# All of the short convolution in the paired products of a hybrid mixer block, six z tiles in its old place, time-step products among the first pairs

## The chip, the core and the metric

The kernel runs on one core of one Trainium2 chip. The metric is the device time of one launch in microseconds (us). TensorE (PE in the profile) does the matrix products, its weight loads are listed apart as PEld; VectorE (DVE), ScalarE (ACT) and GpSimd (POOL) do elementwise work; SyncE (SP) only issues DMA transfers. ACT and POOL can issue transfers as well. Each engine runs its own list of instructions in order, and waits on semaphores for the others.

## The reference

One layer over 1024 rows of 1024 channels, in float32: a mixer with two branches, then a feed-forward part (hidden size 2816), with normalisations. The mixer, cut to what matters:

```python
u = rmsnorm(x) @ w_in          # 1024 x 10272
z, xbc, dt_raw, s_b, s_c, s_x, g_a, g_b = split(u)   # 2048, 3072, 32, then 1024 each
xbc = silu(causal_conv4(xbc) + bias)            # x, B, C of the scan
dt  = softplus(dt_raw + dt_bias)                # "time steps", 32 heads
y   = ssd_scan(x, dt, a, B, C) + d_skip * x     # 32 heads in 4 groups
y   = group_rmsnorm(y * silu(z)) * ssd_norm_w
v   = causal_conv3(s_c * s_x)                   # the short convolution
merged = sigmoid(g_a) * (y @ w_ssd_proj) + sigmoid(g_b) * ((s_b * v) @ w_sconv_proj)
h = h + merged @ w_o
```

## The kernel before

**Products.** Every float32 operand is split into a high part (written by ACT) and a low part (the difference, written by DVE), and a product is three matmuls: high by high, high by low, low by high (`mm3`, `mmc`, lines 81 to 83 and 663 to 665). A weight slab of 128 columns is a page of 128 x 8 x 128; all large tiles are pages out of one pool of 47, and all product sums lie in eight banks of PSUM.

**First stage, pairs.** 29 pairs of 128-column tiles of `w_in` are computed by a scheme with seven products in place of eight (`Pair`, `ORDER`; its sums of operands are T1 to T4 on the activation side, S1 to S4 on the weight side). One product of one pair is a slot: twelve matmuls. The first three pairs (six z tiles) go product by product through 21 slots, while `second_half()` still makes the second half of the normalised rows and T1, T2, T3, B22 and T4 out of it; the table `turns` says behind which slot it takes a step. The other 26 pairs follow one after the other, a pair with a convolution of the scan's inputs and one of the list `free_p` by turns. Before, `free_p` holds nine pairs of the short convolution (channels 0 to 767 of s_c, s_x, s_b) and then five pairs of z. What follows a pair (silu, convolution, store to DRAM) is a generator in the list `side`, and `pump()` takes one step of one generator per slot. Copies between DRAM buffers for later stages (`v_sums`, and in the next stage `y_sums`, which also works on DVE) are generators in `aux`, taken by `pump_aux()`, here at every seventh slot.

**Time steps.** `steps_pe()` at slot 25 splits a small slab of 32 columns, makes the d_skip columns, and issues 60 matmuls into two banks; `time_steps` works on from there.

**Second stage, direct tiles and scan.** 22 tiles of 128 columns are computed plainly in `direct_tile`: two halves of 24 matmuls. Before, the first six are the last 256 channels of s_c, s_x and s_b, with their short convolution made on DVE and ACT out of PSUM; sixteen gate tiles follow, which ACT copies out of PSUM and stores by its own DMA queue. Between these matmuls the scan runs: 32 items (4 groups by 8 chunks of 128 rows), each with `part1` (transposes, decay matrix) and `part2` (products with the state), one step about every fifth group of matmuls. ACT makes the decay with Exp in `prep2` (line 390 on). The x rows of a half group are loaded by `want(.., 2)` (line 363) in `part1` of the last chunk before they are used. The slab of tile i + 2 is loaded at step (1, 0) of tile i; its high part is made at (0, 1) and its low part at (0, 7) of tile i + 1.

**Third stage on.** `Stream` runs the merge products in chunks: `ahead(loads, splits)` says how many chunks have been loaded and split. Then come the output product and the feed-forward part; the change leaves them alone.

Of the kernel before, what the change touches and what calls it, by code (L numbers as in the profile page):

```python
# [13 lines left out]
P = 128  # L14
# [25 lines left out]
def hybrid_block(ctx: ExitStack, tc: tile.TileContext, x, nmw, w_in, cw, cb, dtb, alog, dsk, snw,  # L40
# [186 lines left out]
    wdt_s = wslab(w_in, DT0, H)  # L227
# [396 lines left out]
    def conv_sb(j):  # L624
        def f(u):
            v = held.pop(j)
            V.tensor_mul(v, u, v)
# [290 lines left out]
    z_pairs = [Pair(i * P, (silu_z(i), silu_z(i + 1))) for i in range(0, 16, 2)]  # L918
# [3 lines left out]
    sc_pairs = [Pair(c0 + j * P, (f(j), f(j + 1))) for j in (0, 2, 4)  # L922
# [46 lines left out]
    direct = []  # L969
    for j in (6, 7):  # L970
        hold = {}

        def d_sc(ps, hf, hold=hold):
            if hf == 0:
                hold[0] = page("sc")
            nc.scalar.activation(hold[0][:, hf * 512:hf * 512 + 512], ps, AF.Copy)

        def d_sx(ps, hf, hold=hold, j=j):
            sc, o = hold[0], slice(hf * 512, hf * 512 + 512)
            V.tensor_mul(sc[:, o], ps, sc[:, o])  # L980
            if hf:
                v = hold[0] = page("v")
                nc.scalar.activation(v, sc, AF.Copy, scale=scc(2, j))
# [4 lines left out]
        def d_sb(ps, hf, hold=hold, j=j):  # L988
            v, o = hold[0], slice(hf * 512, hf * 512 + 512)
            V.tensor_mul(v[:, o], ps, v[:, o])  # L990
            if hf:
# [22 lines left out]
    def direct_tile(i):  # L1014
# [3 lines left out]
        for hf in range(2):  # L1018
            ps = bank("pr")
            for k in range(KT):  # L1020
# [15 lines left out]
                if i + 2 < len(direct) and (hf, k) == (1, 0):  # L1036
# [489 lines left out]
    for p in first[1:]:  # L1526
        p.y.load()
    for p in first:
        p.x.load()
    loaded[0] = NF  # L1530
    wdt_s.load()
# [36 lines left out]
    def second_half():  # L1568
# [19 lines left out]
        yield  # L1588
        for k in range(2):
# [3 lines left out]
        yield  # L1593
        every(put("B22", raw1[1]))
# [7 lines left out]

    gen = second_half()
# [104 lines left out]
```

## Time and profile before

| | |
|---|---|
| time of three runs | 1981.1, 1982.43 (median), 1985.02 us |
| profiled execution | 1979.01 us, span 1977.2 us |
| mean granted clock of TensorE | 0.984 |
| busy: PE, DVE, ACT, POOL | 1908.5, 1299.5, 960.8, 177.1 us |
| first pairs | about 20 to 110 us of the span |
| other pairs | about 110 to 617 us |
| direct tiles and scan | about 617 to 1006 us |

The page splits the span in 40 slices and gives the busy share of each engine in tenths, and the clock that TensorE was granted. Views of the trace give the same for any window, the waits of one engine by what ended them, the instructions in order of time, and the DMA issues. A wait row reads: engine, tile and line that waited, what it waited for, total us, number, longest. A group row reads: line, engine, operation, tiles and shapes, count, busy us, mean ns of one, and the idle time before.

### The profile page before, as it was taken

What the parts mean: (1) busy time and instruction counts of PE and PEld (TensorE: products, weight loads), DVE (VectorE), ACT (ScalarE), POOL (GpSimd) and SP (SyncE); (2) the same over time, 40 slices, a digit from 0 to 9 for tenths busy, and PEclk for the clock granted to TensorE, in tenths of its full rate; (3) what the DMA queues carried; (4) which work ended last, traced back from release to release, by engine and by line L of the source; (5) the groups of instructions that cost most, each with busy time, mean ns of one, the idle gap of its engine ahead of it and who ended that gap; (6) DMA issues with size and microseconds to landing.
All of it is one profiled execution on the core that took longest, in us unless ns stands there. A gap on an engine that the chain in (4) does not pass through costs nothing.

```text
span 1977.2 us, 24421 instructions
## 1 busy us (share of the span) xinstructions
PE 1908.5 (97%) x8917; PEld 1563.3 (79%) x8917; DVE 1299.5 (66%) x1678; ACT 960.8 (49%) x1526; POOL 177.1 (9%) x156
## 2 busy tenths in 40 slices
PE   6899999999999998999999999989999999999998
PEld 4678888888887876887878888878888888878886
DVE  6747878778765886887958557867444444455465
ACT  5534444444457766776546544355333333335433
POOL 0000101010100111111200000101121112100000
PEclk8899999999999998998999999999999999999999
DMA  5176989799975649687789866843989788868553
GB/s 175 35 202 156 234 228 238 206 245 249 257 214 181 187 151 276 229 255 234 249 312 406 289 213 207 219 139 80 237 190 207 209 195 194 211 236 306 199 183 116
DMA packets 350833, 422.49 MB, mean 214 GB/s; under 512 B 19752, under 2 KB 226424, under 8 KB 350712
## 3 DMA queue, kind: packets, MB, share of 16 engines
q1 hardware_dynamic: 305112, 356.95, 54.9%
q0 software_dynamic: 43296, 55.58, 17.6%
q10 hardware_dynamic: 2304, 8.39, 1.1%
q8 instruction: 70, 1.15, 0.2%
q14 instruction: 51, 0.42, 0.1%
HBM read 328.95 MB, written 145.24 MB: 240 GB/s over the span
## 4 chain that ended last, share of the span: by engine, by line
PE 58%; DVE 3%; DMA 1%; ACT 1%; issue 0%; SPq 0%; DVEq 0%; ACTq 0%
PE gb L664 5%; PE gb L665 5%; PE gb L663 5%; PE fb L665 4%; PE fb L664 4%; PE fb L663 4%; PE gd L665 4%; PE gd L664 4%; PE gd L663 4%; PE fd L665 3%; PE fd L663 3%; PE fd L664 3%; PE pr L81 3%; PE pr L83 3%; PE pr L82 3%; PE pdg L483 1%
## 5 line engine op out<-in xcount | busy, mean ns | idle before, releaser
L77 DVE TENSOR_TENSOR wl<-ws,wh 128x1024 fp32r<-128x1024 f32 (+1 forms) x78 | 94.4, 1211 | 123.2 <-ACT wh L76 123.2
L664 PE MATMUL gb<-ql,gh 128*128 128x512 f32 x432 | 169.6, 393 | 4.1 <-DVE ql L77 4.1
L663 PE MATMUL gb<-qh,gh 128*128 128x512 f32 x432 | 169.6, 393 | 3.2 <-ACT qh L76 3.2
L665 PE MATMUL gb<-qh,gl 128*128 128x512 f32 x432 | 169.0, 391 | 0.0
L83 PE MATMUL pr<-th,wl 128*128 128x512 f32 x352 | 139.9, 397 | 6.9 <-DVE wl L1011 6.9
L81 PE MATMUL pr<-th,wh 128*128 128x512 f32 x352 | 146.3, 416 | 0.0
L663 PE MATMUL fb<-th,wh 128*128 128x512 f32 x352 | 138.5, 393 | 2.6 <-ACT th L76 2.0
L82 PE MATMUL pr<-tl,wh 128*128 128x512 f32 x352 | 139.9, 397 | 0.0
L665 PE MATMUL fb<-th,wl 128*128 128x512 f32 x352 | 138.0, 392 | 0.8 <-DVE wl L77 0.8
L664 PE MATMUL fb<-tl,wh 128*128 128x512 f32 x352 | 138.2, 393 | 0.5 <-DVE tl L77 0.5
L663 PE MATMUL gd<-qh,gh 128*128 128x512 f32 x324 | 126.0, 389 | 0.0
L664 PE MATMUL gd<-ql,gh 128*128 128x512 f32 x324 | 126.0, 389 | 0.0
L665 PE MATMUL gd<-qh,gl 128*128 128x512 f32 x324 | 126.0, 389 | 0.0
L76 ACT ACTIVATE qh<-cb 128x1024 fp32r<-128x1024 f32 x98 | 100.0, 1020 | 39.2 <-PE gb L664 17.2
L77 DVE TENSOR_TENSOR ql<-cb,qh 128x1024 fp32r<-128x1024 f32 x98 | 115.6, 1180 | 2.4 <-ACT qh L76 2.1
L665 PE MATMUL fd<-th,wl 128*128 128x512 f32 x264 | 102.7, 389 | 0.0
L663 PE MATMUL fd<-th,wh 128*128 128x512 f32 x264 | 102.7, 389 | 0.0
L664 PE MATMUL fd<-tl,wh 128*128 128x512 f32 x264 | 102.7, 389 | 0.0
L74 DVE SCALAR_TENSOR_TENSOR gl<-ca,gh 128x1024 fp32r<-128x1024 f32 (+1 forms) x60 | 70.5, 1174 | 45.0 <-ACT gh L73 45.0
L664 PEld LDWEIGHTS gb<-ql,gh 128*128 128x128 f32 x432 | 81.8, 189 | 21.6 <-DVE ql L77 4.7
L663 PEld LDWEIGHTS gb<-qh,gh 128*128 128x128 f32 x432 | 81.9, 190 | 20.9 <-ACT qh L76 3.9
L665 PEld LDWEIGHTS gb<-qh,gl 128*128 128x128 f32 x432 | 81.8, 189 | 17.1
(310 smaller groups left out, 4711.3 us busy)
## 6 DMA issues: line engine op xcount, KB each, us to landing
ws<-in_w_in_dram SPq DMA_DIRECT2D x80, 512.0 KB, 7.8
ws<-in_w_gate_dram SPq DMA_DIRECT2D x77, 256.0 KB, 3.7
ws<-in_w_up_dram SPq DMA_DIRECT2D x77, 256.0 KB, 4.2
ca<-u_d SPq DMA_DIRECT2D x35, 512.0 KB
ab<-ac_d SPq DMA_DIRECT2D x32, 512.0 KB, 5.6
xbc_d<-cv SPq DMA_DIRECT2D x24, 512.0 KB, 3.4
ws<-ws POOLq DMA_DIRECT2D x22, 512.0 KB, 6.5
wd_d<-in_w_down_dram SPq DMA_DIRECT2D x20, 512.0 KB, 8.7
```

The lines of the kernel that those rows point to most:

```text
L74: nc.vector.scalar_tensor_tensor(lo, src, -1.0, hi.bitcast(F32), op0=ALU.mult, op1=ALU.subtract)
L76: nc.scalar.activation(hi, src, AF.Copy)
L77: nc.vector.tensor_sub(lo, src, hi.bitcast(F32))
L81: nc.tensor.matmul(o, lh, rh, start=first, stop=False)
L82: nc.tensor.matmul(o, lh, rl, start=False, stop=False)
L83: nc.tensor.matmul(o, ll, rh, start=False, stop=last)
L483: nc.tensor.matmul(pdg[64 * i:64 * i + 64, r * P:(r + 1) * P], xx[:, 0, 2 * r + i, :], ab[:, 2 * r + i, :], start=True, stop=True)
L663: nc.tensor.matmul(o, lh, rh, start=first, stop=False, skip_group_check=True)
L664: nc.tensor.matmul(o, lh, rl, start=False, stop=False, skip_group_check=True)
L665: nc.tensor.matmul(o, ll, rh, start=False, stop=last, skip_group_check=True)
```

## The change

- The list `free_p` now begins with all twelve pairs of the short convolution; the z pairs beyond the first three are cut from five to two. The copies `v_sums` are started from the pairs for both halves, and `pump_aux()` comes at every third slot instead of every seventh.
- The first six direct tiles are now z tiles 10 to 15 (`z_raw`): ACT applies Silu to each half straight out of PSUM and stores the tile by its own DMA queue.
- The slab of the time steps is loaded ahead of the first x slabs and split before slot 0; its 24 and 36 matmuls stand behind slots 5 and 11. `second_half()` makes B22 before T3. The d_skip columns move to slot 35.
- The slab of direct tile i + 2 is loaded at step (0, 2) instead of (1, 0), and the merge chunks are loaded and split one chunk sooner.

TensorE, first pairs. `pd_` tiles are sums of pairs, `ts_` is the sum of the time steps; `th`, `tl` are the parts of the activations. Before, behind slot 5:

```order
L663 MATMUL pd_541<-th_370,wh_378 128x512
L664 MATMUL pd_541<-tl_371,wh_378 128x512
L665 MATMUL pd_541<-th_370,wl_379 128x512
L663 MATMUL pd_559<-th_533,wk_495 128x512
L664 MATMUL pd_559<-tl_534,wk_495 128x512
L665 MATMUL pd_559<-th_533,wk_495 128x512
```

Now, at the same place:

```order
L663 MATMUL pd_545<-th_370,wh_378 128x512
L664 MATMUL pd_545<-tl_371,wh_378 128x512
L665 MATMUL pd_545<-th_370,wl_379 128x512
L663 MATMUL ts_563<-th_316,wdt_384 32x512
L664 MATMUL ts_563<-tl_317,wdt_384 32x512
L665 MATMUL ts_563<-th_316,wdt_385 32x512
```

24 rows of `ts` now stand ahead of the first row that reads T1 (`th_533` before), and 36 more ahead of slot 12.

ScalarE, first direct tile: `cd`, `ab` are the decay of the scan (Exp), `pr` is the sum of a direct tile, `st` the state of the scan. Before:

```order
L390 ACTIVATE cd_4634<-ab_4535 128x8
L392 ACTIVATE ab_4535<-ab_4535,pac 128x128 x8
L394 ACTIVATE ab_4535<-ab_4535 128x1024
L976 ACTIVATE sc_4655<-pr_4588 128x512
L476 ACTIVATE st_4666<-pst_4667 128x512
L430 ACTIVATE bh_4717<-pcb_4713 128x128
L434 ACTIVATE xw_4720<-xx_4716 128x512
L448 ACTIVATE y_4528<-bc_4530,cols 128x128 x2
L448 ACTIVATE y_4529<-x_561_4451,cols 128x128 x2
L390 ACTIVATE cd_4733<-ab_4607 128x8
```

Now:

```order
L390 ACTIVATE cd_4646<-ab_4544 128x8
L392 ACTIVATE ab_4544<-ab_4544,pac 128x128 x8
L394 ACTIVATE ab_4544<-ab_4544 128x1024
L975 ACT_TABLE_LOAD
L975 ACTIVATE gt_4667<-pr_4598 128x512
L476 ACTIVATE st_4676<-pst_4677 128x512
L430 ACTIVATE bh_4727<-pcb_4723 128x128
L434 ACTIVATE xw_4730<-xx_4726 128x512
L448 ACTIVATE y_4537<-bc_4539,cols 128x128 x2
L448 ACTIVATE y_4538<-x_562_4459,cols 128x128 x2
L390 ACT_TABLE_LOAD
L390 ACTIVATE cd_4743<-ab_4619 128x8
```

A table load now stands ahead of the Silu of a z tile and another ahead of the next Exp. In the whole list of ACT there are 43 table loads where there were 24.

SyncE, second stage, ahead of the x rows of chunk 4 of the second group (`x_` from `xbc_d`). Before:

```order
L992 DMA v_g_166<-v_5447 128x1024
L381 DMA eb_5661<-e_d 64x4x128 x2
L539 DMA y_g_161<-y_4528 128x512 x2
L680 DMA vt_d_210<-v_g_165 256x512
L680 DMA vt_d_211<-v_g_166 256x512
L680 DMA vt_d_212<-v_g_165 256x512
L680 DMA vt_d_213<-v_g_166 256x512
L363 DMA x_781_5695<-xbc_d_126 128x512
L363 DMA x_781_5695<-xbc_d_127 128x512
```

Now:

```order
L165 DMA ws_5643<-in_w_in_dram 128x8x128
L381 DMA eb_5673<-e_d 64x4x128 x2
L539 DMA y_g_162<-y_4537 128x512 x2
L363 DMA x_785_5703<-xbc_d_127 128x512
L363 DMA x_785_5703<-xbc_d_128 128x512
```

The store of `v` and the four copies into `vt_d` are gone from here; they now stand in the first stage, ahead of the last z stores of the pairs, and the four accumulating copies that POOL issues for them follow there too.

The diff, cut:

```diff
-    wdt_s = wslab(w_in, DT0, H)
+    wdt_s = sp.tile([P, KT * H], F32, tag="eb", name="wdts").rearrange("p (k h) -> p k h", h=H)
...
-            if j % 4 == 1 and j > 4:
-                aux.append(v_sums(0))
+            if j in (5, 7):
+                aux.append(v_sums(j - 5))
...
-    z_pairs = [Pair(i * P, (silu_z(i), silu_z(i + 1))) for i in range(0, 16, 2)]
+    z_pairs = [Pair(i * P, (silu_z(i), silu_z(i + 1))) for i in range(0, 10, 2)]
...
-    sc_pairs = [Pair(c0 + j * P, (f(j), f(j + 1))) for j in (0, 2, 4)
+    sc_pairs = [Pair(c0 + j * P, (f(j), f(j + 1))) for j in (0, 2, 4, 6)
                 for c0, f in ((SC0, conv_sc), (SX0, conv_sx), (SB0, conv_sb))]
...
-        def d_sx(ps, hf, hold=hold, j=j):
-            sc, o = hold[0], slice(hf * 512, hf * 512 + 512)
-            V.tensor_mul(sc[:, o], ps, sc[:, o])
+    def z_raw(i):
+        hold = []
+
+        def f(ps, hf):
+            if hf == 0:
+                hold.append(page("gt"))
+            nc.scalar.activation(hold[0][:, hf * 512:hf * 512 + 512], ps, AF.Silu)
             if hf:
-                v = hold[0] = page("v")
-                nc.scalar.activation(v, sc, AF.Copy, scale=scc(2, j))
-                for sh in (1, 2):
-                    V.scalar_tensor_tensor(v[:, sh:], sc[:, :S - sh], scc(2 - sh, j), v[:, sh:],
-                                           op0=ALU.mult, op1=ALU.add)
...
-                nc.sync.dma_start(v_d[j], v)
-                if j == 7:
-                    aux.append(v_sums(2))
-        direct += [(wslab(w_in, SC0 + j * P), d_sc), (wslab(w_in, SX0 + j * P), d_sx), (wslab(w_in, SB0 + j * P), d_sb)]
+                nc.scalar.dma_start(z_d[i], hold.pop())
+        return f
+
+    direct = [(wslab(w_in, i * P), z_raw(i)) for i in range(10, 16)]
...
-                if i + 2 < len(direct) and (hf, k) == (1, 0):
+                if i + 2 < len(direct) and (hf, k) == (0, 2):
                     direct[i + 2][0].load()
...
+    def wdt_split():
+        for d in range(2):
+            t = sp.tile([P, 512], F32R, tag="st", name=nm("wdt"))
+            wdt_hl.append(t[:, 0:KT * H].rearrange("p (k h) -> p k h", h=H))
+        nc.scalar.activation(wdt_hl[0], wdt_s, AF.Copy)
+        V.tensor_sub(wdt_hl[1], wdt_s, wdt_hl[0].bitcast(F32))
+
+    def steps_pe(hf):
+        wh, wl = wdt_hl
+        ps = bank("ts")
+        todo = [(n, k, k0 + k) for n, k0 in ([("B11", 0), ("B21", 4)], [("B11", 0), ("T1", 0), ("B22", 4)])[hf]
+                for k in range(4)]
+        for j, (n, k, kw) in enumerate(todo):
+            bh, bl = half_b(n, k)
+            mmc(ps[:H], wh[:, kw, :], wl[:, kw, :], bh, bl, j == 0, j == len(todo) - 1)
+        steps_ps.append(ps)
...
+    wdt_split()
     gen = second_half()
-    turns = {0: 2, 1: 2, 2: 2, 3: 2, 4: 1, 6: 1, 8: 1, 11: 1, 14: 1}
+    turns = {0: 2, 1: 2, 2: 2, 3: 2, 4: 1, 6: 1, 8: 1, 10: 1, 14: 1}
...
+        if i == 2 * NF - 1:
+            steps_pe(0)
+        if i == 4 * NF - 1:
+            steps_pe(1)
...
         if i == 7 * NF + 4:
-            steps_pe()
+            time_steps(steps_ps)
+            del steps_ps[:]
+        if i == 7 * NF + 14:
+            d_skip_columns()
...
-        if i % 7 == 5:
+        if i % 3 == 1:
             pump_aux()
...
         direct_tile(i)
-        ms.ahead(i - len(direct) + 3, i - len(direct) + 1)
+        ms.ahead(i - len(direct) + 4, i - len(direct) + 2)
```

More of the change, by code (lines that the diff above doesn't have):

```diff
@@ L1527, in hybrid_block @@
         p.y.load()
+    nc.sync.dma_start(wdt_s, w_in[:, DT0:DT0 + H].rearrange("(k p) f -> p k f", p=P))
     for p in first:
@@ L1530, in hybrid_block @@
     loaded[0] = NF
-    wdt_s.load()
     a0 = rows_sq(xt[0:4], "x", "avav")
@@ L1588, in second_half @@
         yield
+        every(put("B22", raw1[1]))
+        yield
         for k in range(2):
@@ L1592, in second_half @@
         raw1[0].clear()
-        yield
-        every(put("B22", raw1[1]))
         raw1[1].clear()
@@ L1620, in steps_pe @@
         V.tensor_copy(cols[:, 176:192], pd2[:, 0:16])
-        wh, wl = wdt_s.split()
-        wdt_s.hl = None
-        ps = [bank("ts") for _ in range(2)]
-        seq = [("B11", 0), ("B21", 4)], [("B11", 0), ("T1", 0), ("B22", 4)]
-        for hf in range(2):
-            todo = [(n, k, k0 + k) for n, k0 in seq[hf] for k in range(4)]
-            for j, (n, k, kw) in enumerate(todo):
-                bh, bl = half_b(n, k)
-                mmc(ps[hf][:H], wh[:, kw, :], wl[:, kw, :], bh, bl, j == 0, j == len(todo) - 1)
-        time_steps(ps)
     sums = all_weight_sums()
```

15 lines of the change are left out of this document (3 added, 12 removed).

## The prediction

> **What bounds the kernel now.** I read the busy line and the slices first, then windows of 40 us, then TensorE's waits, and last the list of the engine that was waited for. TensorE bounds it: it is busy 1908.5 of 1977.2 us. What can be won is in the few slices below 9, and in those where the clock is down.
>
> ```profile
> PE   6899999999999998999999999989999999999998
> PEclk8899999999999998998999999999999999999999
> ```
>
> In the windows (the first number of each pair is the busy time, in brackets the instructions; then PEld, DVE, ACT, POOL, the granted clock, the DMA share, GB/s) a full 40 us of the pairs holds 179 matmuls at clock 1.00, so one costs 0.223 us.
>
> ```profile
> 40.00:80.00 40.00, 36.05 (x150) 28.79 (x150) 30.13 (x37) 19.02 (x28) 0.00 (x0) 0.91 0.13 40
> 80.00:120.00 40.00, 36.37 (x152) 29.22 (x151) 22.63 (x27) 21.79 (x28) 2.38 (x4) 0.96 0.54 181
> ...
> 560.00:600.00 40.00, 40.00 (x179) 33.10 (x178) 27.23 (x33) 19.29 (x27) 2.46 (x4) 1.00 0.57 158
> 617.00:720.00 103.00, 99.44 (x587) 80.48 (x586) 79.03 (x123) 73.91 (x178) 10.91 (x4) 0.98 0.54 166
> 720.00:760.00 40.00, 29.26 (x155) 23.21 (x154) 26.87 (x45) 26.84 (x69) 2.66 (x3) 0.83 0.84 235
> 920.00:960.00 40.00, 35.59 (x188) 28.98 (x188) 31.66 (x57) 25.61 (x63) 4.75 (x2) 0.87 0.72 241
> 1000.00:1040.00 40.00, 35.44 (x149) 28.64 (x148) 24.37 (x27) 20.39 (x23) 0.00 (x0) 0.96 0.91 334
> ```
>
> A wait is paid twice here: the window that holds it also shows a lower clock. At 720 to 760 the clock of 0.83 costs 0.17 x 40 = 6.8 us beside the wait. TensorE's waits, from 40 to 120 us, from 617 to 760 and from 900 to 1040:
>
> ```profile
> PE pb L665 <- DVE wl L877: 2.9, 1, 2.9
> PE pb L665 <- DVE wk L877: 2.0, 1, 2.0
> PE pd L663 <- ACT th L76: 1.1, 1, 1.1
> PE pd L664 <- DVE tl L77: 0.8, 1, 0.8
> ```
>
> ```profile
> PE pxt L420 <- DMA x<-xbc_d: 9.2, 2, 7.2
> PE poff L469 <- ACT st L476: 2.6, 2, 1.8
> PE pr L83 <- DVE wl L1011: 2.5, 3, 1.2
> ```
>
> ```profile
> PE pr L83 <- DVE wl L1011: 4.4, 1, 4.4
> PE gb L663 <- ACT qh L76: 3.2, 1, 3.2
> PE gb L664 <- DVE ql L77: 1.4, 1, 1.4
> ```
>
> **The change, part by part.** The number of matmuls stays the same: three pairs of z become three of the short convolution, six direct tiles stay six, and the 60 time-step matmuls only move. So the sum is one of waits.
>
> *Time steps among the first pairs.* The waits of 40 to 120 us sit ahead of slot 6 (T1: `th`, `tl`), in slot 11 (`wk`) and in slot 14 (`wl`), 6.8 us together. Clocks of 0.91 and 0.96 cost 0.09 x 40 + 0.04 x 40 = 5.2 us. Now 24 matmuls (24 x 0.223 = 5.4 us) stand ahead of slot 6 and 36 (8.0 us) ahead of slot 12. The first batch is longer than the 1.9 us of T1, and what is left of it delays TensorE for `wk` by about its 2.0 us too; the second is longer than 2.9 us. DVE also does less ahead of `wk`, since B22 (no subtraction) comes before T3. The new work that ACT and DVE get here is one split of a 256-column slab. I take the whole 12.0 us. The bounds are 0 (DVE, busy 30.1 of 40 us, simply ends later) and 12.0. The slab's transfer goes ahead of three x slabs on SP's queue; it is 128 KB, and the x slabs are first wanted at slot 2. The d_skip transpose keeps its wait on DVE at its new slot: 0.
>
> *Short convolution in the pairs.* Each 128 channels cost DVE two products and two shifted additions and ACT one scaling; the silu of six z tiles goes from ACT.
>
> ```profile
> L619 DVE SCALAR_TENSOR_TENSOR v<-u,cols,v 128x1023 f32<-128x1023 f32 (+1 forms) x12 | 15.3, 1278 | 0.2 <-ACT v L616 0.2
> L627 DVE TENSOR_TENSOR v<-u,v 128x1024 f32<-128x1024 f32 x6 | 7.3, 1218 | 0.0
> ```
>
> For two of them that is 2 x (2 x 1.22 + 2 x 1.28) = 10.0 us more DVE, spread over the last six pairs. From 560 to 600 us DVE was idle 12.8 of 40 us, and the nine such pairs before ran at 40.00 of 40 us. I take 0; were that cover gone, up to 3 us, about one low part late with its clock.
>
> *The copies leave the scan.* SP's own list around the 9.2 us:
>
> ```profile
> 735.48 1.06 SPq L539 DMA_DIRECT2D y_g<-y  x2
> 736.60 3.23 SPq L680 DMA_DIRECT2D vt_d<-v_g  x4
> 739.93 1.75 SPq L363 DMA_DIRECT2D x<-xbc_d  x2
> ```
>
> TensorE at the same time, the first transposes and the two that wait:
>
> ```profile
> 742.25 0.38 PE L420 MATMUL pxt<-ident,bc 128*128 128x128 f32 x2
> 749.84 0.47 PE L420 MATMUL pxt<-ident,x 128*128 128x128 f32 x1 [7.21 <-DMA x<-xbc_d]
> 752.31 0.48 PE L420 MATMUL pxt<-ident,x 128*128 128x128 f32 x1 [2.00 <-DMA x<-xbc_d]
> ```
>
> And another load of that size, from the list of DMA issues (count, size, median us to landing):
>
> ```profile
> z<-z_d SPq DMA_DIRECT2D x32, 256.0 KB, 4.7
> ```
>
> The x rows are issued 2.3 us before they are wanted, behind four copies of 512 KB, and take 10 us to land; the other load of 256 KB lands in 4.7 us. Without the copies they go out at 736.6, and with 1.75 us for issuing and 4.7 us to land they are there at 743.1, about 0.5 us late. So 9.2 + 6.8 - 0.5 = 15.5 us go. If only the 3.3 us of issue time went and the DMA engines stayed as full, 5.9 us of waiting would stay, with clock in the same ratio (6.8 / 9.2 = 0.74) 10.3 us, and 5.7 us go. I take 15.5: DMA share was 0.84 in that window, with the 2 MB of copies in it. In the pairs the copies run beside a share of 0.57, and nobody waits for them before the merge.
>
> *Z tiles on ACT.* This is the cost. The list of ACT gains 19 table loads, nearly all in the first six direct tiles.
>
> ```profile
> L390 ACT ACT_TABLE_LOAD x7 | 9.0, 1283 | 0.1
> L640 ACT ACTIVATE gt<-pr 128x512 f32<-128x512 f32 x32 | 18.6, 585 | 24.3 <-PE pr L83 24.3
> ```
>
> ```profile
> L983 ACT ACTIVATE v<-sc,cols x2: 1152/1152/1152, 656.5 to 711.8; 128x1024 f32<-128x1024 f32 x2
> ```
>
> Loads 19 x 1.283 = 24.4 us, twelve evictions 12 x 0.585 = 7.0, less four evictions (2.3) and two scalings (2.3): 26.8 us. From 617 to 720 us ACT was busy 73.9 of 103 us, so it would be at 100.7: nearly full, but not over. What its idle time was there:
>
> ```profile
> ACT bh L430 <- PE pcb L424: 14.1, 4, 5.7
> ACT xw L434 <- DVE xx L431: 7.2, 4, 4.4
> ACT v L983 <- DVE sc L980: 6.3, 2, 3.9
> ```
>
> The 6.3 us go with the short convolution; the other 21.3 us are slack in the sense that ACT had caught up, and a later ACT fills them. Where it had not caught up, a load is paid in full:
>
> ```profile
> 633.11 1.28 ACT L390 ACT_TABLE_LOAD   x1
> 634.40 0.22 ACT L390 ACTIVATE cd<-ab 128x8 f32<-128x8 f32 x1
> ...
> 638.10 0.58 ACT L976 ACTIVATE sc<-pr 128x512 f32<-128x512 f32 x1
> 638.58 0.59 ACT L476 ACTIVATE st<-pst 128x512 f32<-128x512 f32 x1
> ```
>
> The state copy at 638.58 is what `poff` waits 1.8 us for, and a load now stands before it. Behind a late ACT, DVE is late with `bh` and then with the low part `wl`. I charge one load to each of these two, with its clock: 2 x 1.28 x 1.74 = +4.5 us. The bounds are -4.4 (the 2.5 us of `wl` waits go with their clock, as DVE is freed of two short convolutions here) and +33 (none of the 21.3 us filled: ACT needs 122 us, 19 over, 19 x 1.74).
>
> *Loads a stage sooner.* The 4.4 us at 926 come from DVE waiting in `y_sums` for its own loads; that order is the same: 0, and -9.6 if it goes with its clock (4.4 + 0.13 x 40). In the merge ACT still splits chunk 0 behind the last eviction, only DVE's part moves ahead of two row scalings: -0.5, at most -6.2 (3.2 + 1.4 + 0.04 x 40).
>
> Sum: -12.0 - 15.5 + 4.5 - 0.5 = -23.5 us. The profiled execution took 1979.0 us; it becomes 1955.5. The median of the runs shown is 3.4 us above the profiled one, so **1959 us**.
>
> **Rivals.**
>
> *ACT becomes the bound of the first six tiles.* For it: 100.7 of 103 us. If half of the 21.3 us of waiting can't be filled, ACT needs 111.4 us, 8.4 over; with clock 14.6 us stand in place of 4.5: 1969. Against it: those waits appear only after ACT had caught up. Chance 0.17.
>
> *The x rows are late all the same,* behind row stores that wait for a late DVE: 5.7 instead of 15.5 us gone, 1969. For it: they are issued only 2.3 us ahead. Chance 0.10.
>
> *The time steps fill nothing,* because DVE is the bound of the first pairs: 12.0 us stay, 1971. Against it: DVE was idle 9.9 us from 40 to 80. Chance 0.05.
>
> *Slower: the z stores hold ACT.* Each z tile puts a transfer into ACT's list, and such an issue can wait for other transfers:
>
> ```profile
> 742.37 0.58 ACT L640 ACTIVATE gt<-pr 128x512 f32<-128x512 f32 x1
> 746.91 0.34 ACTq L642 DMA_DIRECT2D ga_d<-gt  x1
> ```
>
> Here ACT stood 4.0 us behind an eviction. Six such stops are 24 us, ACT is 22 us over, with clock at 1.74 that is 38 us in place of 4.5: 1992. It turns the sign when ACT is more than 28 / 1.74 = 16 us over, so from 3.1 us per store. Against it: that stop fell among the copies that leave. Chance 0.06.
>
> *Slower: a table load stops ACT for longer than its row,* as long again at the bound: 24.4 us more, ACT 22.1 us over, 38 us in place of 4.5 and 1992 again. Against it the row above: the load starts at 633.11, lasts 1.28, and the next instruction starts at 634.40. Chance 0.02. The Trainium skill, ScalarE: Activation LUTs, What ACT_TABLE_LOAD costs, states about 1283 ns for the load and about 1380 ns more for emptying the engine, 2.66 us per switch; by that 19 switches would cost 50 us, and this case would be the outcome. The trace agrees with the load and shows no such stop behind it.
>
> **How the numbers follow.** The forecast has 0.60, with 1945 (ACT costs nothing and the wait at 926 goes too) to 1967 as its own range. 1946 to 1977 holds it with the first three rivals and leaves the slower ones out. A change under 0.2% (4 us) can't be told from none here. Faster: 0.60 + 0.10 + 0.05 + 0.12 of the first rival = 0.87; the same: 0.05 of the first, should more than half stay unfilled; slower: 0.06 + 0.02 = 0.08.
>
> **What would show it.** From 40 to 120 us TensorE busy near 80 us at clock 1.00, and no `wl`, `wk`, `th` waits; the `ts` matmuls there. No wait of `pxt` for x rows above 1 us in the direct tiles. 43 table loads, ACT above 90% busy from about 605 to 708 us, and `poff` waiting for `st` about 3 us. I am wrong in the main if those six tiles hold more than 10 us of TensorE waits, or if a wait for x rows stays.

## The result, and the profile after

The changed kernel takes **1964.62 us** (median of four runs, 1961.5 to 1966.51) beside 1981.76 us for the kernel before on the same chip: a ratio of 0.9909, 95% interval 0.989 to 0.9928. It is 17 us faster; the forecast was 1959 us with a range of 1946 to 1977, so the direction was right and the forecast time 5.6 us too low. The profiled execution took 1965.9 us, span 1964.1, so 13.1 us less than the one before (1979.0), where the sum of the prediction had 23.5. Executions of one kernel mostly differ by 3 to 9 us, so terms are compared inside the profiled executions, and whole kernels by their medians.

First the places where TensorE stands at the seams of the stages: the last product of the pairs ahead of the scan, the scan's first transposes, the first product of a direct tile, the first of the merge. Before (start, length, instruction, and in brackets what it waited for):

```profile
614.03 0.40 PE L665 MATMUL pd<-th,wl 128*128 128x512 f32 x1
614.26 0.39 PE L420 MATMUL pxt<-ident,bc 128*128 128x128 f32 x2
...
617.78 0.39 PE L81 MATMUL pr<-th,wh 128*128 128x512 f32 x1
...
1009.64 0.50 PE L663 MATMUL gb<-qh,gh 128*128 128x512 f32 x1 [3.20 <-ACT qh L76]
```

After:

```profile
604.66 0.39 PE L665 MATMUL pd<-th,wl 128*128 128x512 f32 x1
609.09 0.82 PE L420 MATMUL pxt<-ident,bc 128*128 128x128 f32 x2 [4.05 <-DMA bc<-xbc_d]
...
616.46 0.40 PE L81 MATMUL pr<-th,wh 128*128 128x512 f32 x1
...
997.09 0.50 PE L663 MATMUL gb<-qh,gh 128*128 128x512 f32 x1 [3.09 <-ACT qh L76]
```

The pairs end 9.4 us sooner. Between them and the first direct tile 8.1 us are lost again (11.8 us in place of 3.75). The direct tiles take 380.6 us in place of 391.9, so 11.2 less. Behind them 0.5 us more are saved.

| stretch, profiled executions | predicted | measured |
|---|---|---|
| pairs | -12.0 | -9.4 |
| pairs to first direct tile | 0 | +8.1 |
| direct tiles and scan | -15.5 + 4.5 = -11.0 | -11.2 |
| merge and later | -0.5 | -0.5 |
| sum | -23.5 | -13.0 |

The direct tiles and the merge came out as forecast in sum (the parts of the direct tiles did not, as is shown further down), and the gap of 10.5 us lies in the first two rows. The windows of the changed kernel (columns as in the prediction; the last line is the kernel before from 600 to 617 us):

```profile
40.00:80.00 40.00, 38.85 (x179) 27.76 (x178) 29.78 (x36) 19.55 (x27) 0.00 (x0) 1.00 0.13 38
80.00:120.00 40.00, 40.00 (x178) 32.34 (x177) 21.20 (x26) 20.62 (x27) 2.38 (x4) 1.00 0.53 174
...
600.00:617.00 17.00, 12.60 (x45) 9.45 (x44) 5.53 (x7) 7.64 (x14) 1.62 (x2) 0.80 1.09 293
617.00:720.00 103.00, 99.67 (x588) 81.29 (x587) 69.48 (x115) 97.87 (x201) 10.58 (x4) 0.97 0.59 193
720.00:760.00 40.00, 38.81 (x242) 31.30 (x241) 30.79 (x56) 33.05 (x71) 1.32 (x1) 1.00 0.70 218
...
600.00:617.00 17.00, 17.00 (x80) 14.15 (x79) 7.45 (x10) 8.33 (x11) 0.00 (x0) 1.00 0.76 232
```

From 40 to 120 us TensorE is busy 78.9 of 80 us at full clock, and from 720 to 760 us 38.8 of 40 where it had 29.3. ScalarE is busy 97.9 of 103 us in the first six direct tiles. New is the stretch of 600 to 617 us: DMA share 1.09 and a clock of 0.80, where the kernel before had 0.76 and 1.00.

TensorE's waits of the changed kernel, first from 40 to 140 us, then from 600 to 720, then from 900 to 980:

```profile
PE pb L665 <- DVE wk L877: 1.8, 2, 1.1
PE pb L663 <- ACT u L899: 1.5, 1, 1.5
```

```profile
PE pxt L420 <- DMA bc<-xbc_d: 4.0, 1, 4.0
PE poff L469 <- ACT st L476: 3.2, 1, 3.2
PE pxt L420 <- DMA x<-xbc_d: 0.4, 2, 0.2
```

```profile
PE pr L83 <- DVE wl L996: 6.8, 1, 6.8
```

The wait of 9.2 us for x rows is gone; the 0.4 us above belong to other x rows, at the scan's start. In its place stand 4.0 us for the scan's first B and C rows at 609 us, 1.5 and 0.7 us at 133 us, and the wait for `wl` that took 4.4 us at 927 us takes 6.8 us at 915 us. Around such a stop the granted clock is 0.50 for some us; what is called a half-clock stretch below costs half of the time that TensorE is busy in it.

**Where the 4.0 us come from.** SP's list of the changed kernel ahead of the scan:

```profile
581.17 4.52 SPq L680 DMA_DIRECT2D vt_d<-v_g  x4
...
587.85 4.03 SPq L597 DMA_DIRECT2D z_d<-u  x2
591.92 0.65 SPq L165 DMA_DIRECT2D ws<-in_w_in_dram  x1
592.67 9.15 SPq L359 DMA_DIRECT2D bc<-xbc_d  x4
```

POOL adds the accumulating copies of the same `vt_d` at 586.6, 591.8, 599.9 and 608.3 us. The first of the four issues for `bc` stands 6.2 us, and the rows land 8.0 us after their issue, where they took 5.9 before (one landing is known in each trace). The copies left the x rows and now stand ahead of the B and C rows.

**Where the wait at 133 us comes from.** ScalarE and VectorE of the changed kernel in the time steps:

```profile
129.90 0.42 ACT L302 ACTIVATE ts<-ts 128x256 f32<-128x256 f32 x1 [7.85 <-DVE ts L301]
130.22 0.58 ACT L914 ACTIVATE u<-pb 128x512 f32<-128x512 f32 x1
```

```profile
129.44 0.42 DVE L301 SCALAR_TENSOR_TENSOR ts<-ts 128x256 f32<-128x256 f32 x1 [4.33 <-DMA ts<-tr]
```

The sums of the time steps are moved from `tr` to `ts` by four transfers on SP (issued from 120.6 us). ScalarE stands 7.9 us until VectorE has them, and the evictions of the pair queue up. Before, TensorE had its 60 time-step matmuls at this place (120 to 134 us): the first two of the four transfers went out under them, at 127.1 us, and ScalarE stood only 3.3 us. So a transfer that the matmuls covered came to light; it was also slower here, which isn't told apart. That this chain makes the wait is shown below: the wait goes when the chain comes two steps later.

**Where the 6.8 us come from.** VectorE of the changed kernel ahead of that wait, in `y_sums` (L720, L721):

```profile
903.71 0.69 DVE L720 TENSOR_TENSOR bt<-br 128x512 f32<-128x512 f32 x1 [5.72 <-DMA br<-y_g]
905.55 0.69 DVE L721 TENSOR_TENSOR bt<-bt,br 128x512 f32<-128x512 f32 x1 [1.14 <-DMA br<-y_g]
907.58 0.69 DVE L431 TENSOR_TENSOR xx<-pxt,wdt 128x512 f32<-128x512 f32 x1 [1.34 <-DMA yt_d<-bt]
...
914.11 1.22 DVE L996 TENSOR_TENSOR wl<-ws,wh 128x1024 fp32r<-128x1024 f32 x1
```

### The profile page after: what moved, and what is told of

Same layout as the page of the kernel before. It is cut to its first block, busy times and chain, and to the rows that moved or that the text cites. A ratio compares the mean times of both kernels' runs of the same rounds, so it can differ in the third digit from the quotient of the medians.

```text
span 1964.1 us, 24428 instructions
## 1 busy us (share of the span) xinstructions
PE 1903.3 (97%) x8917; PEld 1560.3 (79%) x8917; DVE 1294.5 (66%) x1674; ACT 984.2 (50%) x1547; POOL 176.4 (9%) x156
## 4 chain that ended last, share of the span: by engine, by line
PE 55%; DVE 3%; DMA 2%; ACT 2%; issue 1%; SPq 0%; ACTq 0%; DVEq 0%
PE gb L664 5%; PE gb L665 5%; PE gb L663 5%; PE fb L665 4%; PE fb L664 4%; PE fb L663 4%; PE gd L665 4%; PE gd L664 4%; PE gd L663 4%; PE fd L663 3%; PE fd L664 3%; PE fd L665 3%; PE pr L81 2%; PE pr L83 2%; PE pr L82 2%; PE pdg L483 1%
## 5 line engine op out<-in xcount | busy, mean ns | idle before, releaser
L77 DVE TENSOR_TENSOR wl<-ws,wh 128x1024 fp32r<-128x1024 f32 x77 | 94.0, 1222 | 123.2 <-ACT wh L76 123.2
L76 ACT ACTIVATE qh<-cb 128x1024 fp32r<-128x1024 f32 x98 | 100.0, 1020 | 40.7 <-PE gb L664 17.2
```

Of the source, the lines that this page charges most:

```text
L76: nc.scalar.activation(hi, src, AF.Copy)
L77: nc.vector.tensor_sub(lo, src, hi.bitcast(F32))
```

## The experiments

All medians beside the kernel before on the same chip; ratios with 95% intervals. Differences between two kernels carry the error of both, some 4 to 5 us. For comparison the changed kernel: 0.9909 (0.989 to 0.9928).

### The time steps undone

```diff
-        if i == 2 * NF - 1:
-            steps_pe(0)
-        if i == 4 * NF - 1:
-            steps_pe(1)
...
-            time_steps(steps_ps)
...
+            steps_pe()
```

> The changed kernel with the part on the time steps undone: the slab of the time steps loaded behind the x slabs, its 60 matmuls at slot 25, B22 behind T3, the d_skip columns at slot 25. My prediction put this part at 12.0 us: by it 1964.6 becomes 1976 to 1977. My reading of the two traces: from 0 to 120 us the change took 5.7 us of waits and 13.7 us at half clock (6.8 us), but new waits of 1.5 and 0.7 us with 3.4 us at half clock stand at 133 us, because TensorE no longer has those 60 matmuls while the time steps' transfer is under way; so the pairs end 9.4 us later here and the time is 1974. Rival: what the pairs lose, the wait for B and C rows at 609 us and the waits behind it give back in part, since transfers and VectorE have longer to catch up: 1966 to 1970.

Measured: 1977.03 us, ratio 0.9973 (0.9961 to 0.9985), so 12.4 us above the changed kernel (8 to 17 by the two intervals). The waits of 40 to 120 us are back (`wk`, `wl`, `th`, `tl`), those at 133 us are gone, and the wait for `bc` is still there with 4.5 us: nothing was given back behind the pairs. By the medians the part is worth what the prediction said, 12 us. My own reading of the trace (9.4, so 1974) was too low by what followed behind the pairs: in the profiled executions the first direct tile starts 8.0 us later, the merge 9.9, and the whole takes 10.6 us more. So the near match with 12.0 is in part chance.

### The copies of the kernel before, moved; and then the additions of y_sums too

First only the copies, from direct tile 6 to tile 9 of the kernel before:

```diff
-                if j == 7:
-                    aux.append(v_sums(2))
...
+                if (i, hf, k) == (9, 1, 0):
+                    aux.append(v_sums(2))
```

> The kernel before, with only the copies that sum the last 256 channels of v moved, from direct tile 6 (about 736 us) to the second half of direct tile 9 (about 785 us). It takes from the change the one term that I put at 15.5 us. My theory: TensorE's 9.2 us of waiting for x rows at 742 to 752 us and the 13.7 us at half clock behind them come from those copies alone: 9.2 + 6.8 - 0.5 = 15.5 us less, 1981.8 becomes 1966. Rival: the x rows are late all the same: 5.7 us less, 1976. Second rival: the copies make a like collision at their new place with the next x rows: 1980.

Measured: 1975.47 us, ratio 0.9974 (0.9959 to 0.9989): 5 us, not 15.5. TensorE's waits from 720 to 760, 760 to 900 and 900 to 980 us:

```profile
PE pxt L420 <- DMA x<-xbc_d: 0.3, 1, 0.3
...
PE pr L83 <- DVE wl L1009: 1.9, 1, 1.9
PE pxt L420 <- DMA x<-xbc_d: 0.8, 1, 0.8
...
PE pr L83 <- DVE wl L1009: 7.5, 1, 7.5
```

The x rows are in time, as the theory had it, but the gain is not kept. Counting direct tiles from 0, tile 7 takes 17.2 us in place of 29.3, so 12.1 us were won there. Tile 12 takes 22.8 us in place of 17.5, with the new wait at 826 us, and tile 17 takes 30.9 in place of 28.0, as the wait behind VectorE's stop in `y_sums` grows by 3.1 us. What makes the wait at 826 us is not shown: in the next experiment the copies stand at the same place, and it is not there. So in the second experiment the four additions in `y_sums` come two steps behind their loads:

```diff
             yield
+            yield
             t = page("bt", HB)
...
-            yield
             V.tensor_add(r1[:, 1, :], r1[:, 1, :], r2[:, 1, :])
```

> The kernel before with two edits: the v copies moved to direct tile 9 (which alone gave 1975.5 where I expected 1966), and the four additions of y_sums two steps behind their loads. In the run with the copies moved alone the 9.2 us wait for x rows was gone, but a wait for wl at 917 us grew from 4.4 to 7.5 us and a new one of 1.9 us with 6.8 us at half clock stood at 826 us. Theory: TensorE that is no longer stopped at 742 us runs into the next late engine, VectorE in y_sums, and the rest of the 15.5 us comes out when that stop is taken away too: 7.5 + 6.8 = 14.3 us less, 1961 to 1963. Rival: VectorE or ScalarE as such set the pace of these tiles, and the wait only moves again: 1970 or more.

Measured: 1969.12 us, ratio 0.9938 (0.9918 to 0.9957). That is 6 us more than the copies alone, less than half of what was expected; the runs lie from 1964 to 1973. In the profiled execution (1964.2 us) the direct tiles take 376.8 us, where the kernel before had 391.9 and the copies alone 387.0, and the largest wait from 760 to 980 us is 2.9 us. So the stop is worth taking away, but that the rest of the 15.5 us was held back by it is not shown: the edit of `y_sums` alone was not run on the kernel before, and on the changed kernel it gives 7.1 us alone (next experiment). Two gains of 5 and 7 us that simply add would come to nearly the same.

### The same edit of y_sums on the changed kernel

> The changed kernel, with the four additions of y_sums all made two steps behind their loads, where two of them came one step behind and two at the second step; the number of steps is the same. My theory: VectorE stands 5.7 + 1.1 us in y_sums at 898 to 905 us for rows whose load went out 0.4 us before, and so TensorE waits 6.8 us for the low part wl at 915 and runs 10.2 us at half clock. With the additions a step later these waits go: 6.8 + 5.1 = 11.9 us less, 1964.6 becomes 1953. Rival: VectorE is the bound there by its own work, and the wait only shrinks by what the wait for the store (1.3 us) is worth: about 1962. Second rival: the four additions in one block (2.7 us) make wl late elsewhere: 1960 or more, with a new wait of TensorE for wl between 870 and 1000 us.

Measured: **1957.51 us**, ratio 0.9876 (0.9859 to 0.9894), 7.1 us below the changed kernel. The wait for `wl` fell from 6.8 to 1.2 us; the direct tiles take 373.1 us in place of 380.6. Some small waits came up (`pq`, `prt`, `st`, 0.9 to 1.2 us each), and 2.4 of the 10.2 us at half clock had lain within the wait itself and were counted twice in the 11.9; so not all of it came out. Of the kernels that compute the whole layer this one and the one with one copy per step, below, are the fastest; both beat the changed kernel.

### The copies later in the changed kernel

```diff
-            if j in (5, 7):
-                aux.append(v_sums(j - 5))
+            if j == 5:
+                aux.append(v_sums(0))
...
+                if (i, hf, k) == (1, 1, 0):
+                    aux.append(v_sums(2))
```

> The changed kernel, with the copies that sum the last 256 channels of v started from the second half of direct tile 1 (about 640 to 650 us) and not from the last pairs. My theory: those copies (2 MB by SP, 2 MB by POOL from 581 us on) fill the DMA engines while the first B and C rows of the scan are loaded, so TensorE waits 4.0 us for bc at 609 us and runs 6.8 us at half clock behind it. Then that wait falls below 1 us, its half-clock stretch goes, and 4.0 + 3.4 = 7.4 us go: 1964.6 becomes 1957. Rival: the rows are late because SP is held by something else (stores of z that wait for a late ScalarE); then the wait stays near 4 us and the time near 1965. Second rival: at their new place the copies delay the state's or the next x rows there; then a new wait of some us for x or bc stands between 640 and 690 us, and the time is 1960 to 1965.

Measured: 1966.17 us, ratio 0.9919 (0.9902 to 0.9935), no gain. The first direct tile starts at 608.0 us in place of 616.5, so the wait for `bc` was the copies' work, and 8.5 us were won there. The merge starts at 997.3 in place of 997.1. The second rival of the expectation came out, with another load than I named. TensorE from 617 to 720 us, and ScalarE behind the copies:

```profile
PE pr L83 <- DVE wl L996: 4.0, 2, 3.5
PE poff L469 <- ACT st L476: 3.3, 1, 3.3
```

```profile
664.00 1.28 ACT L390 ACT_TABLE_LOAD   x1
670.02 0.21 ACT L390 ACTIVATE cd<-ab 128x8 f32<-128x8 f32 x1 [4.73 <-DMA ab<-ac_d]
```

The decay rows `ab` of a chunk came 4.7 us late, in the tiles where ScalarE is busy 97.9 of 103 us in the changed kernel.

### The silu of the direct z tiles left out

```diff
-            nc.scalar.activation(hold[0][:, hf * 512:hf * 512 + 512], ps, AF.Silu)
+            nc.scalar.activation(hold[0][:, hf * 512:hf * 512 + 512], ps, AF.Copy)
```

> The changed kernel, with the six direct z tiles copied out of PSUM and stored without their silu (this leaves out the silu of 768 of the 2048 z channels). The table loads that the change added in the first six direct tiles go, some 19 of 1.28 us, and nothing else. My prediction charged them 4.5 us: two loads of 1.28 us on the path with their clock. By that the wait of poff for st at 637 us falls from 3.2 to about 1.9 us, its half-clock stretch from 6.8 to 3.4 us, and 1964.6 becomes 1960 to 1962. Rival: ScalarE is the bound of these tiles and all 24 us of loads press on it: 10 us or more go, 1955 or less. Rival: the loads are hidden wholly: 1965.

Measured: 1962.43 us, ratio 0.9896 (0.9877 to 0.9914): 2.2 us below the changed kernel by the medians, which the intervals cannot tell from none. The number of table loads is back at 24. In the trace the wait for `st` fell from 3.2 to 1.0 us and its half-clock stretch of 6.8 us went, 5.6 us together. The first six direct tiles take 98.7 us, where the executions with the table loads, and without copies beside them, have 101.1 to 104.6 (104.0 in the changed kernel). So the price of the table loads lies between 2 and 6 us, where 4.5 was predicted; that ScalarE bounds these tiles (10 us or more) is out. The kernel before, without these loads but with the short convolution there, has 103.6 us, and 102.0 in its two variants: what left these tiles gave 3 to 5 us back, and the prediction had that as a bound only.

### The loads put back

```diff
-                if i + 2 < len(direct) and (hf, k) == (0, 2):
+                if i + 2 < len(direct) and (hf, k) == (1, 0):
...
-        ms.ahead(i - len(direct) + 4, i - len(direct) + 2)
+        ms.ahead(i - len(direct) + 3, i - len(direct) + 1)
```

> The changed kernel with the loads put back: slab of tile i + 2 at step (1, 0), merge chunks loaded and split one chunk later. My prediction put this part at -0.5 us: 1965. Rival: the loads a stage sooner are what lengthened the wait for wl from 4.4 us at 927 to 6.8 us at 915 (a slab more on SP ahead of the y rows, and one page less for them); then that wait is back near 4.4 us and the time is 1960. Second rival: without them slabs come late in the direct tiles, new waits for wl or wh: 1970.

Measured: 1968.98 us, ratio 0.9939 (0.9924 to 0.9954), 4.4 us above the changed kernel. The wait for `wl` stays at 6.4 us, so the sooner loads did not lengthen it. At the merge's start TensorE waits 3.2 and 2.1 us (3.1 and 0.9 after the change) with 6.8 us at half clock in place of 3.4: 3.0 us. The part is worth 3 us by the trace and 4 to 6 by the medians and ratios, inside the bound of 6.2 and not at the 0.5 I took.

### Three edits together

The additions of `y_sums`, two more steps ahead of the time steps' chain, and the scan's first loads sooner:

```diff
         def rest():
             yield
+            yield
+            yield
...
+        if left == 7:
+            pump_scan()
...
-        if left == 4:
-            pump_scan()
```

> The changed kernel with three edits: additions of y_sums two steps behind their loads (alone 7.1 us), the elementwise chain of the time steps two steps later, so that it does not hold ScalarE and VectorE while its transfer is under way (the waits of 1.5 and 0.7 us at 133 us with their 3.4 us at half clock: 3.2 us less), and the first loads of the scan three slots (8 us) sooner, ahead of most of the v copies (the wait of 4.0 us for bc with 6.8 us at half clock: 7.4 us less). If these add up: 1964.6 - 7.1 - 3.2 - 7.4 = 1947. Rival: as where the copies were moved away from the scan's start (8.5 us won by 608 us, all lost by 997 us), what is won ahead of the direct tiles is lost in the first six of them, where ScalarE has no idle time: 1954 to 1958, with new waits for wl or st between 617 and 720 us.

Measured: 1963.5 us, ratio 0.9913 (0.9899 to 0.9927), 6 us worse than `y_sums` alone. The waits at 133 us went, and the one for `bc` fell to 1.9 us. But the slab of the first direct tile now stands behind the scan's loads on SP's queue:

```profile
614.16 1.06 ACT L995 ACTIVATE wh<-ws 128x1024 fp32r<-128x1024 f32 x1 [14.69 <-DMA ws<-in_w_in_dram]
```

TensorE waits 4.1 us for its high part and 6.5 for a low part behind it. The DMA share was 1.05 from 590 to 600 us and 1.03 from 600 to 615: in this window the new order only chose which load was late.

### One copy per step; the silu late; x rows early

With the additions of `y_sums` and the chain of the time steps as above, the copies go one per step from direct tile 3:

```diff
                 nc.sync.dma_start(f[i + 1], blk_of(*first[i]))
+                if apart:
+                    yield
...
+                if (i, hf, k) == (3, 1, 0):
+                    aux.append(v_sums(2, True))
```

> The changed kernel with the additions of y_sums two steps behind their loads, the chain of the time steps two steps later, and the copies for the last 256 channels of v started at direct tile 3 (about 676 us), one copy per step (8.6 us) in place of four at once. The scan's first loads stay where they are. If the terms add up (7.1 for y_sums as measured alone, 3.2 at 133 us, 7.4 at the scan's start): 1947. Rival: ScalarE has no idle time in the first six direct tiles, so that what is won ahead of them is lost there: 1954 to 1958, with TensorE waiting 5 us or more for wl and st between 610 and 720 us.

Measured: 1957.07 us, ratio 0.9875 (0.9854 to 0.9896), the same as `y_sums` alone. The scan starts at 602.2 us without a wait, and TensorE waits 0.6 us for `wl` and 3.2 for `st` from 617 to 720 us. So ScalarE doesn't take the gain back; at 733 us the x rows do, behind the copies:

```profile
PE pxt L422 <- DMA x<-xbc_d: 5.3, 2, 5.1
```

Beside that, the silu moved to the loaded rows:

```diff
+        for i, t in enumerate((zs, z)):
+            if 4 * g + 2 * i >= 10:
+                nc.scalar.activation(t, t, AF.Silu)
```

> The same kernel, and beside it the six direct z tiles stored as they come out of PSUM, with their silu applied to the rows that the third and fourth group of the scan load again (six activations of 128 x 1024 after 840 us, where ScalarE is busy 65 to 75%). This takes the table loads between z tiles and decays out of the first six direct tiles. If ScalarE is what takes the gain back there, the waits for wl and st between 610 and 720 us fall below 3 us and the time is 6 to 10 us below the kernel without this edit: 1945 or less. If ScalarE is not the cause: within 2 us of it. If the activations at 840 to 980 us make VectorE or the group norm late: slower than it, with waits for wl, pq or prt there.

Measured: 1960.99 us, ratio 0.9895 (0.9877 to 0.9913), slower by 4 us by the medians, on the same chip. `st` fell to 1.8 us as expected. Behind 900 us stand `st` with 2.9 us (at 950 us) and `wl` with 2.1 (at 900 us), and 17 us at half clock: the third branch of the expectation. The wait for x rows is still there, with 3.3 us from 720 to 760 us.

Or, in place of that, the x rows a chunk sooner:

```diff
         if c % 4 == 2:
...
+            want(j // 4 + 1, 2)
...
-        if c % 4 == 3:
-            want(j // 4 + 1, 2)
```

> The kernel with one copy per step from direct tile 3 (1957.1), and the x rows of a half group loaded in the same step as its first B and C rows, one chunk (about 12 us) sooner than now. In that kernel TensorE waited 5.3 us for x rows at 733 us with 6.8 us at half clock behind it, while the copies were under way; the x rows are issued some 2 us before they are wanted. Theory: it is this short lead that turns any copy beside it into a wait; with 12 us more of lead the wait falls below 1 us and 5.3 + 3.4 = 8.7 us go: 1948 to 1950. Rival: with the wait gone the next late engine takes the gain back (VectorE's low part, the group norm), as in the two kernels where a stall at the scan's start was taken away: 1955 to 1957. Second rival: the page that the rows hold for 12 us longer makes slabs late: new waits for wh or wl, 1957 or more.

Measured: 1959.54 us, ratio 0.9885 (0.9866 to 0.9905). The wait for x rows is gone, and these stand in its place, from 720 to 760 and from 900 to 980 us:

```profile
PE pq L522 <- DVE sa L517: 4.6, 1, 4.6
...
PE pr L83 <- DVE wl L1001: 3.1, 1, 3.1
```

### The copies without their dependence

```diff
-            if j in (5, 7):
-                aux.append(v_sums(j - 5))
+            if j == 5:
+                aux.append(v_sums(0))
+                aux.append(weight_sums("T", vt_d, [(v_g[0], 0, v_g[1], 0, 2 * P, 256)]))
```

> The changed kernel with the additions of y_sums two steps behind their loads and the chain of the time steps two steps later, and with the copies of the last 256 channels of v replaced by copies of the first ones, made directly behind the first batch (about 490 to 520 us): the same traffic, but without the dependence that puts it at the end of the pairs. This leaves out the last 256 channels of the sums for the short convolution's product, so it only bounds what the place of the copies is worth. If the copies at the scan's start cost their wait with its clock (4.0 + 3.4 us) and nothing takes it back: y_sums alone gave 1957.5, 3.2 us go at 133 us and 7.4 at 609 us, 1947. If the second stage's own pace (ScalarE full in the first six tiles, then the chain of the group norm) takes back what is won ahead of it: 1954 to 1957, with the pairs ending near 605 us and the last direct tile no sooner than 984 us.

Measured: 1951.83 us, ratio 0.9846 (0.9824 to 0.9869). This kernel leaves out the sums of the last 256 channels, so it is a bound and no candidate. The direct tiles take 374.7 us, as with `y_sums` alone (373.1), though they start 7.5 us sooner. It lies between the two cases: most of what is won ahead of the direct tiles stays won, so it isn't the pace of the second stage that took the gain back in the runs above, but the copies themselves, at their next place. In every place that was tried the right copies cost 5 us or more beside this.

## Why the prediction was right, and where not

**Time steps, -12.0: right in the mechanism.** Undone, the kernel is 12.4 us slower by the medians, 10.6 in the profiled executions. The waits of 40 to 120 us went but for 1.1 us at `wk`, and the half-clock stretches there with them; that they fill nothing fell as a rival. What was missed is the step "the 60 time-step matmuls only move": they also covered part of the transfer of the time steps' own chain, and 1.5 + 0.7 us with 3.4 us at half clock came up at 133 us. That takes 3.9 of the 12.0 us back in the pairs' account.

**Short convolution in the pairs, 0: right at its place.** From 560 to 600 us TensorE is busy 40.00 of 40 us and VectorE 27.9, where it had 27.2.

**The copies, -15.5: the step that failed.** The wait for x rows did go (9.2 us to none from 720 to 760 us), as reckoned from the load of like size, and the rival by which they are late all the same fell. The sentence "nobody waits for them before the merge" was wrong: the scan's first rows are loaded in the same 25 us. I had read the DMA share of a window of the pairs (0.57 from 560 to 600 us), and not what is issued right behind the copies' new place. That cost 4.0 us and 3.4 by the clock, the larger part of the 8.1 us. And the term was reckoned as if what TensorE no longer waits at 742 us stayed won: the copies' move alone gave 5 us on the kernel before.

The term was also too large at its own place. Direct tile 7, which holds the stop, took 29.3 us before, and 17.2 in the changed kernel as well as with the copies alone moved: 12.1 us, not 15.5. The sum added half of the whole half-clock stretch (6.8 us) to the wait, but the clock fell while TensorE still stood. The kernel before:

```profile
745.00:759.00 14.00, 7.16 (x23) 5.90 (x24) 4.22 (x9) 5.04 (x16) 1.77 (x2) 0.51 1.08 301
```

TensorE was busy only 7.2 of these 14.0 us, so the clock cost about 3.6 us and not 6.8.

**The wait at 926 us, 0: the second step that failed.** I took it to stay, since the order there is the same. It stayed, and grew by 2.4 us; VectorE's stop ends by a load, and that load went out 7.1 us behind the start of direct tile 16 (897.7 us) where it had gone out 3.9 us behind it (908.7 us). Why it went out later stays open; with the sooner slab loads put back the wait is still 6.4 us. As part of the same sentence I had the bound "-9.6 if it goes": it went by a change of two lines, for 7.1 us.

**Z tiles on ACT, +4.5: the loads about right, the term not.** The 43 table loads, ScalarE at 97.9 of 103 us (100.7 reckoned) and `poff` with 3.2 us for `st` (3 forecast) came as written; the price of the loads is 2 to 6 us. But what left these tiles gave 3 to 5 us back, so the first six direct tiles take 104.0 us where they took 103.6. The rivals that made ScalarE the bound, by itself or by its stores, fell: TensorE was busy 99.7 of those 103 us. The stores on ScalarE's queue took 0.33 to 0.34 us each and held nothing.

**The direct tiles together, -11.0 forecast and -11.2 measured: met by errors that cancel.** The same matmuls, from the first of a tile to the first of the next group, in the profiled executions (those first rows stand at 617.78, 721.35, 770.20, 904.78 and 1009.64 us before, and at 616.46, 720.43, 755.04, 890.59 and 997.09 us after):

| direct tiles | before | after | difference | forecast |
|---|---|---|---|---|
| 0 to 5 (z tiles now) | 103.6 | 104.0 | +0.4 | +4.5 |
| 6 and 7 (x rows) | 48.9 | 34.6 | -14.2 | -15.5 |
| 8 to 15 | 134.6 | 135.6 | +1.0 | 0 |
| 16 to 21 (`y_sums`) | 104.9 | 106.5 | +1.6 | 0 |

Of the 14.2 us, 12.1 are tile 7; the other 2.1 are tile 6, which the copies' move alone left as it was. That the sum fits is luck.

**A table load stops ScalarE for longer than its row: fell.** In the 26 loads from 600 to 760 us the next instruction starts 0.01 us behind the end of the load, and the one ahead of it ended 0.02 us before its start (rounded rows can show 0.01 more):

```profile
633.91 1.06 ACT L394 ACTIVATE ab<-ab 128x1024 f32<-128x1024 f32 x1
634.98 1.28 ACT L975 ACT_TABLE_LOAD   x1
636.28 0.60 ACT L975 ACTIVATE gt<-pr 128x512 f32<-128x512 f32 x1
636.77 0.59 ACT L476 ACTIVATE st<-pst 128x512 f32<-128x512 f32 x1
```

From the end of one activation to the start of the next a switch takes 1.31 us. Activations with no load between them overlap by 0.1 us (the last two rows), so it costs about 1.4 us here. The Trainium skill, ScalarE: Activation LUTs, What ACT_TABLE_LOAD costs, has 2.66 us for every switch, 1.28 of them the load. The load agrees (1.28 us); the rest of the page's figure does not show in this kernel.

**Loads a stage sooner, -0.5: too small by the run that undoes it.** 3 us by the trace, inside the bound, though between the kernel before and the changed one the part behind the direct tiles moved by just 0.5. I had left out that a shorter wait at the merge's start also shortens the half-clock stretch.

**What stays open.** Executions of one kernel mostly differ by 3 to 9 us, by 12 with the copies moved in the kernel before (1969.6 to 1982.0) and by 13 in one series of the kernel before (1975.4 to 1988.5), so the price of the table loads isn't settled better than 2 to 6 us. In the profiled executions the change gave 13.1 us, by the medians 17.1; no run tells how much of that difference is chance.

## What to carry to other kernels

When a block of transfers is moved out of one queue place, read what is loaded in the 20 us behind its new place, not the DMA share there: in four places that were tried a load was late behind the copies (x rows twice, B and C rows, decay rows), and a slab was when the order was changed beside them. A removed wait is a gain only up to the next stop; look for the next wait and plan for it too (on the kernel before the copies' move gave 5 us alone and 13 with the edit of `y_sums`; the change gave 17 and 23). And don't add a wait and half of the half-clock stretch beside it before looking how much of the stretch lies within the wait. When matmuls are moved off a place, ask what they were covering there.

## What the runs showed of the hardware

The granted clock after a stop of TensorE falls in fixed steps. Windows of the changed kernel around three of its waits (4.0 us until 609, 6.8 until 915, 1.5 and 0.7 until 134 us):

```profile
609.00:616.00 7.00, 6.55 (x18) 4.79 (x19) 3.84 (x4) 5.11 (x12) 0.18 (x1) 0.52 1.06 276
616.00:623.00 7.00, 7.00 (x36) 5.81 (x35) 4.97 (x9) 6.94 (x19) 0.00 (x0) 1.00 0.80 290
913.00:923.00 10.00, 7.62 (x25) 6.58 (x26) 9.93 (x18) 4.70 (x13) 0.00 (x0) 0.50 0.81 272
134.00:138.50 4.50, 4.18 (x11) 3.34 (x12) 4.40 (x10) 1.31 (x2) 0.00 (x0) 0.62 0.99 188
```

In all profiled executions the stretches at half clock from 40 us on last 3.4, 6.8, 10.2 or 13.7 us, but for the last one, which the end of the program cuts. Within an execution all changes of the clock lie on one grid of 3.413 us: in the changed kernel the stretches begin at 134.77, 609.22, 636.53 and 913.01 us, which is 139, 8 and 81 steps of 3.413 us apart. Behind stops of 5.9 us and more the stretch was 10.2 or 13.7 us. Behind 3.5 to 5.1 us it was 6.8 as a rule (3.4 behind two stops of 4.0, and 10.2 behind the 4.4 us at 923 us of the kernel before). Behind 1.5 to 3.2 us it was nothing, 3.4 or 6.8, and once 10.2 (2.9 us near 950 us in the kernel with the late silu). Even 1.1 and 0.8 us close together brought 3.4 (53 us, the kernel before). The same stop has different prices: the 1.5 us at 133 us brought 3.4 us at half clock in the changed kernel and none with the loads put back. A stretch can begin while TensorE still stands, and that part of it costs nothing more: in the third line above TensorE is busy 7.6 of 10.0 us.

The Trainium skill, TensorE: Matmul & The Clock Gate, What's actually happening, gives a free-running window of 3413 ns; the lengths and the grid agree with it, and so does a price that depends on where a stop falls. Its section HAM oscillation — how this bites in real kernels has as the rule no gaps above about 3.4 us; here single stops of 1.8 us (at 635 us with the loads put back, at 639 us of the kernel before) already brought 3.4 us at half clock.
